# State space scan of a hybrid encoder: the steps' logarithms in the decays' exponents, and the step projection in 64 columns

## The chip, the core and the metric

The kernel runs on one core of a Trainium2 chip. The metric is the device time of one execution in microseconds (us). TensorE (PE) multiplies matrices, with the load of the stationary operand (PEld) as a separate, overlapping instruction; VectorE (DVE), ScalarE (ACT) and GpSimd (POOL) work element by element; SyncE (SP) issues the DMAs. Each engine takes its instructions in order.

## The reference, cut to what matters

One layer of an encoder over two sequences, 512 and 1024 tokens of width 1024, handled together as T = 1536 tokens. Its mixer has differential attention and a bidirectional state space scan side by side, then comes a feed-forward part. The change lies in the scan, which for each direction computes, in chunks of 128 tokens:

```
dt = softplus(dt_raw + dt_bias)                      # 16 heads per direction
xdt = x * dt
a_cum = cumsum(dt * A)                               # A = -exp(a_log)
seg = a_cum[l] - a_cum[s]
Lmat = exp(where(s <= l, seg, -inf))
y_diag = (C B^T * Lmat) @ xdt                        # per chunk and head
states, prev = scan over chunks of B^T (exp(a_cum[-1] - a_cum) * xdt)
y_off = (C @ prev) * exp(a_cum)
y = y_fwd + y_bwd + d_skip * x
```

So the weight of token s on token l in a diagonal block is the product of C·B, of the decay exp(a_cum[l] - a_cum[s]), and of the step dt[s].

## The kernel before

All products of large matrices are made of float32 numbers split into a high and a low part (`split`, `split_panel`): three matmuls (`gemm`, L164 to L166) for each product, hi·hi, hi·lo and lo·hi.

Phase one holds the normalised input hT as three blocks of 512 tokens and projects it: keys and queries (with the first sequence's attention in between), steps (`dtT`), the convolution's channels, z, and the gates. The steps are projected at L526 to L529: three blocks, each of 8 k-blocks by 3 matmuls with 32 stationary columns and 512 moving columns. Each block is copied by ACT into `dtT`.

L580 to L638 (the preamble) transpose `dtT` to token-major (L584), make `dts` = softplus in a polynomial on DVE, the cumulated sums `acm`, and the exponentials `dec`, `wst`, `eac`. Three transposes of `acm` (L627) are split into `ah`, `al` and stored to DRAM as `ac_d`; from there come four fills of `raw` (one buffer, with rows of a constant table `c_neg`) that are copied to `segr`. `segr` and a per-chunk selector `sl` are the two operands of one matmul (L749) that gives seg for four heads with a mask of -1e30 in it.

L670 to L687 run the backward direction's states over the chunks. Then L712 to L779 are the forward scan: 12 chunks by 2 groups (g) by 2 halves (hf, four heads each), 48 halves in all. In a half, for each direction: seg matmul (L749), exp on ACT (L751), one DVE operation that limits the exponential to 1 and multiplies it by the masked C·B of that direction, `cb` (L752). Then GpSimd multiplies the forward tile by `dts` (L756), four DVE operations on 128 columns multiply the backward tile by its `dts` and add the forward tile (L758), and four matmuls with 64 columns (two passes each) multiply the result by x (L762). After the halves come the skip (POOL, L763), the sums on DVE (L764, L770, L774, L775) and the norm (`finish`).

The program's order is made by a planner that takes instructions by priority as its own model of the engines says they are ready (`schedule_with_timeline_sim=True`). So work that stands later in the code is put into the gaps that the planner sees: the z projection (L694, evacuated at L691) runs in the preamble and beside the backward states, and the gates (`gates`, L424 to L435, called at L782: 14 panels by 3 blocks by 24 matmuls of 512 columns) run in the forward scan and after it. The order on each engine is then fixed. Phase two (attention of the long sequence, L785 on) reuses the memory of phase one.

Of the kernel before, what the change touches and what calls it, by code (L numbers as in the profile page):

```python
# [10 lines left out]
F32 = mybir.dt.float32  # L11
I32 = mybir.dt.int32
F32R = mybir.dt.float32r
AF = mybir.ActivationFunctionType
# [4 lines left out]
P = 128  # L19
# [59 lines left out]
def hybrid_trunk_kernel(ctx: ExitStack, tc: tile.TileContext, a: dict, y_prompt, y_sample):  # L79
# [5 lines left out]
    def f(ap):  # L85
        return ap.bitcast(F32)
# [21 lines left out]
    ac_d = dram.tile([2, 24, NH, P], F32, name="ac_d")  # L108
    f_d = dram.tile([8, 2048], F32, name="f_d")
# [58 lines left out]
    def gemm_fm(ps, w, cs, act):  # L168
        hi, lo = w
        gemm(ps, [(hi[:, k, cs], lo[:, k, cs], act[0][:, k, :], act[1][:, k, :]) for k in range(KB)])  # L170
# [5 lines left out]
    def rsqrt(r, v, t):  # L176
        """r = v ** -0.5 for positive v: a first guess from the exponent, then Newton's steps"""
        V.tensor_scalar(r.bitcast(I32), v.bitcast(I32), 1, None, op0=ALU.logical_shift_right)
        V.tensor_scalar(r.bitcast(I32), r.bitcast(I32), -1.0, 1597463007.0, op0=ALU.mult, op1=ALU.add)
        for _ in range(3):  # L180
            V.tensor_mul(t, r, r)
            V.scalar_tensor_tensor(t, t, -0.5, v, op0=ALU.mult, op1=ALU.mult)
            V.scalar_tensor_tensor(r, t, 1.5, r, op0=ALU.add, op1=ALU.mult)
# [31 lines left out]
    def operands(base, SL, h, qk, qr, got):  # L215
        """the bias table, queries and keys of a head, in steps"""
# [114 lines left out]
    def att_scale(g, zq, msq, pool, psp, ptag):  # L331
        """what the rows of attention are multiplied by: 1 / sum of exponentials and the norm"""
        n = zq.shape[-1]
        r, t = [pool.tile([P, 8, n], F32, tag=t_, name=t_, bufs=1) for t_ in ("att_r", "att_t")]
        V.reciprocal(t, zq)
        V.tensor_mul(zq, msq, t)
        V.tensor_mul(zq, zq, t)
        V.tensor_scalar(zq, zq, 1.0, EPS, op0=ALU.mult, op1=ALU.add)
        rsqrt(r[:], zq[:], msq[:])
        V.tensor_mul(r, r, t)  # L340
        ps = psp.tile([P, 512], F32, tag=ptag, name="rt")
        TE.transpose(ps[0:8 * n, 0:P], r[:].rearrange("p h j -> p (h j)"), ident)
        rt = pool.tile([P, P], F32, tag="att_rt", name="rt", bufs=1)
        V.tensor_copy(rt[0:8 * n], ps[0:8 * n, 0:P])
        store(out=r_d[g][:], in_=rt[0:8 * n])
# [14 lines left out]
    with ExitStack() as ph1:  # L360
# [143 lines left out]
        # step sizes and decays, for both directions at once  # L504
# [11 lines left out]
        wd = [wp.tile([P, KB, 32], F32R, tag=t_, name=t_) for t_ in ("whi", "wlo")]  # L516
        raw = staged(rp, [P, KB, 32], (None, w_in[:, DT0:DT0 + 32].rearrange("(a p) c -> p a c", p=P)),
                     tag="wraw")
        split(wd[0][:], wd[1][:], raw[:], "act_dve")
        dtb = sp.tile([32, 1], F32, name="dtb")  # L520
# [4 lines left out]
        dtT = dtp.tile([32, T], F32, name="dtT")  # L525
        for c in range(NCH):  # L526
            ps = acc.tile([P, 512], F32, tag="acc", name="acc")
            gemm_fm(ps[:32], wd, slice(0, 32), hT[c])
            S.activation(out=dtT[:, c * 512:(c + 1) * 512], in_=ps[:32], func=AF.Identity, bias=dtb[:, 0:1])  # L529
# [50 lines left out]
        with tc.tile_pool(name="dp", bufs=1, reuse_waits="tile") as dp, tc.tile_pool(name="dp_ps", bufs=2, space=PSUM) as dps:  # L580
            natural_log_exp()
            ps = dps.tile([P, NT, 32], F32, tag="dps", name="dt_ps")
            for t in range(NT):
                TE.transpose(ps[:, t, :], dtT[:, t * P:(t + 1) * P], ident[:32, :32])  # L584
# [4 lines left out]
            V.tensor_copy(xr, ps)  # L589
# [33 lines left out]
            ah = dp.tile([P, 3, P], F32R, name="ah")  # L623
            al = dp.tile([P, 3, P], F32R, name="al")
            for i in range(3):
                ps = dps.tile([P, P], F32, tag="dps", name="at_ps")
                TE.transpose(ps, acm[:, 4 * i:4 * i + 4, :], ident)  # L627
                S.copy(ah[:, i], ps)
                V.tensor_sub(al[:, i], ps, f(ah[:, i]))
            for i, t_ in enumerate((ah, al)):  # L630
                store(out=ac_d[i].rearrange("(i c) h l -> (c h) i l", i=3), in_=f(t_[:]))
# [80 lines left out]
        for lo_c, hi_c in SEQS:  # L712
            state = [None, None]
            for c in range(lo_c, hi_c):
                sl = sc.tile([SEGK, 2, P], F32R, tag="sl", name="sl")
                acv = [ac_d[s_, 2 * c:2 * c + 2].rearrange("d h l -> h d l") for s_ in range(2)]
# [8 lines left out]
                for g in range(2):  # L725
# [18 lines left out]
                    for hf in range(2):  # L744
                        ms = []
                        for d_ in range(2):
# [5 lines left out]
                            V.scalar_tensor_tensor(m, m, 1.0, cb[:, d_].unsqueeze(1).broadcast_to([P, 4, P]),  # L752
                                                   op0=ALU.min, op1=ALU.mult)
                            ms.append(m)
                        hh = g * 8 + hf * 4
                        G.tensor_mul(ms[0], ms[0], dts[:, c, hh:hh + 4].unsqueeze(2).broadcast_to([P, 4, P]))  # L756
                        for h in range(4):
                            V.scalar_tensor_tensor(ms[0][:, h], ms[1][:, h], dts[:, c, 16 + hh + h:17 + hh + h], ms[0][:, h],  # L758
                                                   op0=ALU.mult, op1=ALU.add)
# [99 lines left out]
    with ExitStack() as ph3:  # L859
# [43 lines left out]
        # the feed-forward's first product by Strassen's scheme in Winograd's form: seven products of half size  # L903
# [295 lines left out]
```

## Time and profile before

| | us |
|---|---|
| median of 3 runs | 3287.25 |
| lowest, highest | 3272.72, 3288.95 |
| span of the profiled execution, first to last instruction | 3277.1 |

The profiled execution's own time is given only by its span; the median lies 10.15 us above it, and that difference is carried along as what lies around the span. The span is one execution on the chip. Busy time of an engine counts the time in which it had an instruction in work; for the PE, ends of matmuls are modelled, so a PE that is busy throughout need not be at its peak. The granted clock is the TensorE clock as a share of 2.4 GHz; its lower level is 0.5 (1.2 GHz).

### The profile page before, as it was taken

The numbers are of one execution on the slowest core, as the hardware profiler recorded it, in microseconds if no ns is written. First come the engines' busy times: TensorE is split into PE (matmuls) and PEld (weight loads), VectorE is DVE, ScalarE is ACT, GpSimd is POOL, SyncE is SP. The second block draws the span as 40 slices with busy tenths as digits, with TensorE's granted clock in tenths as the row PEclk, the third lists the DMA queues.
The fourth block names the chain that finished last, engine by engine and source line by source line (L and its number), as shares of the span: only waits on it lengthen the run. The fifth ranks groups of instructions, "written<-read, shape, count | busy, mean of one in ns | idle before, by whom it ended". The sixth has DMA issues, their size and how long they took to land.

```text
span 3277.1 us, 44930 instructions
## 1 busy us (share of the span) xinstructions
PE 3068.7 (94%) x16688; PEld 2686.3 (82%) x16688; DVE 1887.9 (58%) x3048; ACT 1207.8 (37%) x2249; POOL 1086.4 (33%) x844
## 2 busy tenths in 40 slices
PE   7999999999899899999999888878999899989998
PEld 7988887889787677778888787677999899978787
DVE  5124444455238998277778765676656766642444
ACT  3013333233113333266666623243333333332343
POOL 1003332000244553167657544533333433310100
PEclk9999999999999999999999998888999999999999
DMA  4623332223553443655545146544333333363354
GB/s 145 193 97 114 112 100 76 67 74 108 174 164 124 130 133 118 200 168 172 178 144 182 39 139 221 172 132 154 98 97 106 96 100 99 110 202 94 117 166 131
DMA packets 442528, 430.00 MB, mean 131 GB/s; under 512 B 25324, under 2 KB 359617, under 8 KB 441245
## 3 DMA queue, kind: packets, MB, share of 16 engines
q1 hardware_dynamic: 442309, 427.12, 41.8%
q8 instruction: 132, 2.16, 0.3%
q14 instruction: 87, 0.71, 0.1%
HBM read 315.37 MB, written 120.05 MB: 133 GB/s over the span
## 4 chain that ended last, share of the span: by engine, by line
PE 57%; DVE 14%; DMA 12%; issue 8%; POOL 5%; ACT 4%; SPq 1%; POOLq 0%; DVEq 0%; ACTq 0%
PE acc L164 8%; PE acc L165 8%; PE acc L166 8%; PE mm L164 4%; PE mm L165 4%; PE mm L166 4%; PE d L166 3%; PE d L164 3%; PE d L165 3%; DMA wraw<-in_w_gate_up_dram 2%; DVE m L758 2%; DMA raw<-k_d 2%; DMA araw<-r_d 1%; PE s L290 1%; DVE m L752 1%
## 5 line engine op out<-in xcount | busy, mean ns | idle before, releaser
L164 PE MATMUL acc<-hT,whi 128*128 128x512 f32 (+1 forms) x1080 | 433.6, 402 | 5.8 <-ACT st L434 5.6
L165 PE MATMUL acc<-hT,whi 128*128 128x512 f32 (+1 forms) x1080 | 431.4, 399 | 0.0
L166 PE MATMUL acc<-hT,wlo 128*128 128x512 f32 (+1 forms) x696 | 273.8, 393 | 0.0
L164 PEld LDWEIGHTS acc<-hT,whi 128*128 128x128 f32 (+1 forms) x1080 | 203.6, 189 | 54.8 <-ACT st L434 6.6
L165 PEld LDWEIGHTS acc<-hT,whi 128*128 128x128 f32 (+1 forms) x1080 | 203.9, 189 | 45.6 <-issue 4.2
L296 ACT ACTIVATE pt<-pt,nm 128x1024 f32<-128x1024 f32 (+1 forms) x192 | 193.4, 1008 | 120.6 <-DVE nm L293 116.4
L293 DVE CUSTOM_DVE_ANT_0 pt<-s,tb 128x1024 f32<-128x1024 f32 (+1 forms) x192 | 197.6, 1041 | 64.5 <-PE s L291 51.2
L165 PE MATMUL acc<-wlo,hT 128*128 128x256 f32 x768 | 226.2, 295 | 0.0
L164 PE MATMUL acc<-whi,hT 128*128 128x256 f32 x768 | 224.6, 293 | 0.0
L166 PE MATMUL acc<-whi,hT 128*128 128x256 f32 x768 | 223.9, 292 | 0.0
L166 PE MATMUL d<-dhi,fl 128*128 128x512 f32 x528 | 207.6, 393 | 9.0 <-DVE fl L136 9.0
L164 PE MATMUL d<-dhi,fh 128*128 128x512 f32 x528 | 207.3, 393 | 8.1 <-DVE dlo L136 6.3
L165 PE MATMUL d<-dlo,fh 128*128 128x512 f32 x528 | 207.1, 392 | 0.0
L136 DVE TENSOR_TENSOR fl<-raw,fh 128x896 fp32r<-128x896 f32 (+1 forms) x72 | 85.9, 1195 | 199.7 <-ACT fh L135 199.7
L164 PE MATMUL mm<-op,wy 128*128 128x384 f32 x528 | 178.8, 339 | 10.2 <-ACT op L135 8.7
L166 PE MATMUL mm<-op,wy 128*128 128x384 f32 x528 | 178.7, 338 | 0.9 <-DVE wy L136 0.9
L165 PE MATMUL mm<-op,wy 128*128 128x384 f32 x528 | 178.3, 338 | 0.0
L302 POOL TENSOR_SCALAR pt<-pt,zs 128x512 f32<-128x512 f32 (+1 forms) x96 | 88.5, 921 | 253.9 <-DVE zs L300 212.6
L231 POOL TENSOR_TENSOR ql<-raw,qh 128x512 fp32r<-128x512 f32 x48 | 64.0, 1347 | 300.9 <-ACT qh L228 294.9
L166 PE MATMUL acc<-hT,whi 128*128 128x512 f32 x384 | 159.1, 414 | 0.0
L164 PEld LDWEIGHTS acc<-whi,hT 128*128 128x128 f32 x768 | 148.4, 193 | 8.9 <-issue 8.0
L135 ACT CAST whi<-wraw 128x1024 fp32r<-128x1024 f32 (+2 forms) x76 | 75.8, 1024 | 215.4 <-PE acc L166 99.6
(344 smaller groups left out, 8696.0 us busy)
## 6 DMA issues: line engine op xcount, KB each, us to landing
wraw<-in_w_in_dram SPq DMA_DIRECT2D x60, 512.0 KB
wraw<-in_w_gate_up_dram SPq DMA_DIRECT2D x92, 256.0 KB
raw<-ff_d SPq DMA_DIRECT2D x48, 448.0 KB
wr<-in_w_gate_up_dram SPq DMA_DIRECT2D x80, 256.0 KB
ff_d<-c SPq DMA_DIRECT2D x88, 192.0 KB
g_d<-st SPq DMA_DIRECT2D x48, 256.0 KB
xg<-xs_d SPq DMA_DIRECT2D x48, 256.0 KB
gt<-g_d SPq DMA_DIRECT2D x48, 256.0 KB
```

The lines of the kernel that those rows point to most:

```text
L135: S.copy(hi, raw)
L136: V.tensor_sub(lo, raw, f(hi))
L164: TE.matmul(ps, ah, bh, start=(i == 0), stop=False)
L165: TE.matmul(ps, ah, bl, start=False, stop=False)
L166: TE.matmul(ps, al, bh, start=False, stop=(i == n - 1))
L231: G.tensor_sub(q_l[:, s_], q_r[:, s_], f(q_h[:, s_]))
L290: TE.matmul(sps[:, ks], qh[m][:, qs], km[m][:, ks], start=True, stop=False)
L293: V.tensor_tensor_reduce(out=pt[:], in0=sps[:], in1=tb[:, off:off + SL], scale=-1.0, scalar=3.0e38, op0=ALU.add, op1=ALU.min, accum_out=nm ...
L296: S.activation(out=pt, in_=pt, func=AF.Exp, bias=nm[:, m:m + 1], scale=-1.0, accum_out=(z0, zs[:, 0:1])[m])
L302: G.tensor_scalar(pm[1][:, cb], pm[1][:, cb], zs[:, 1:2], 0.0, op0=ALU.mult, op1=ALU.add)
L752: V.scalar_tensor_tensor(m, m, 1.0, cb[:, d_].unsqueeze(1).broadcast_to([P, 4, P]), op0=ALU.min, op1=ALU.mult)
L758: V.scalar_tensor_tensor(ms[0][:, h], ms[1][:, h], dts[:, c, 16 + hh + h:17 + hh + h], ms[0][:, h], op0=ALU.mult, op1=ALU.add)
```

## The change

The steps' logarithm is taken into the exponent: exp(a_cum[l] - (a_cum[s] - log dt[s])) already holds the factor dt[s]. A second table `ad_d` (a_cum minus log dt, `acl`) is stored beside `ac_d`, and the selector `sl` is filled from it. The multiplications by `dts` in the scan (L756, L758) go; the two masked tiles are added by one DVE operation. The limit of L752 is 3.0e38 instead of 1. The preamble gets the logarithm with one correction step, and three more transposes and two more stores. The step projection has the high and low parts of the weights side by side as 64 stationary columns, so that a block takes 16 matmuls instead of 24; the two halves are added after the transposes (which now also adds the product lo·lo).

```diff
+    ad_d = dram.tile([2, 24, NH, P], F32, name="ad_d")
...
-        wd = [wp.tile([P, KB, 32], F32R, tag=t_, name=t_) for t_ in ("whi", "wlo")]
+        wd = wp.tile([P, KB, 64], F32R, tag="whi", name="wd")
...
-        split(wd[0][:], wd[1][:], raw[:], "act_dve")
-        dtb = sp.tile([32, 1], F32, name="dtb")
+        split(wd[:, :, 0:32], wd[:, :, 32:64], raw[:], "act_dve")
+        dtb = sp.tile([64, 1], F32, name="dtb")
+        V.memset(dtb, 0.0)
...
-        dtT = dtp.tile([32, T], F32, name="dtT")
+        dtT = dtp.tile([64, T], F32, name="dtT")
         for c in range(NCH):
             ps = acc.tile([P, 512], F32, tag="acc", name="acc")
-            gemm_fm(ps[:32], wd, slice(0, 32), hT[c])
-            S.activation(out=dtT[:, c * 512:(c + 1) * 512], in_=ps[:32], func=AF.Identity, bias=dtb[:, 0:1])
+            for i, (k, part) in enumerate((k, part) for k in range(KB) for part in hT[c]):
+                TE.matmul(ps[:64], wd[:, k, :], part[:, k, :], start=i == 0, stop=i == 2 * KB - 1)
+            S.activation(out=dtT[:, c * 512:(c + 1) * 512], in_=ps[:64], func=AF.Identity, bias=dtb[:, 0:1])
...
-            ps = dps.tile([P, NT, 32], F32, tag="dps", name="dt_ps")
+            ps = dps.tile([P, NT, 64], F32, tag="dps", name="dt_ps")
             for t in range(NT):
-                TE.transpose(ps[:, t, :], dtT[:, t * P:(t + 1) * P], ident[:32, :32])
+                TE.transpose(ps[:, t, :], dtT[:, t * P:(t + 1) * P], ident[:64, :64])
...
-            V.tensor_copy(xr, ps)
+            V.tensor_copy(xr, ps[:, :, 0:32])
+            V.tensor_add(xr, xr, ps[:, :, 32:64])
...
-            ah = dp.tile([P, 3, P], F32R, name="ah")
-            al = dp.tile([P, 3, P], F32R, name="al")
-            for i in range(3):
-                ps = dps.tile([P, P], F32, tag="dps", name="at_ps")
-                TE.transpose(ps, acm[:, 4 * i:4 * i + 4, :], ident)
-                S.copy(ah[:, i], ps)
-                V.tensor_sub(al[:, i], ps, f(ah[:, i]))
-            for i, t_ in enumerate((ah, al)):
-                store(out=ac_d[i].rearrange("(i c) h l -> (c h) i l", i=3), in_=f(t_[:]))
+            acl = dp.tile([P, NT, 32], F32, name="acl")
+            V.tensor_scalar(t1, dts, 1.0e-30, 0.0, op0=ALU.max, op1=ALU.add)
+            S.activation(out=t2, in_=t1, func=AF.Ln)
+            S.activation(out=u, in_=t2, func=AF.Exp, scale=-1.0)
+            V.tensor_mul(u, u, t1)
+            V.scalar_tensor_tensor(t2, u, -1.0, t2, op0=ALU.add, op1=ALU.add)
+            V.tensor_sub(acl, acm, t2)
+            ah = dp.tile([P, 2, 3, P], F32R, name="ah")
+            al = dp.tile([P, 2, 3, P], F32R, name="al")
+            for j, a_ in enumerate((acm, acl)):
+                for i in range(3):
+                    ps = dps.tile([P, P], F32, tag="dps", name="at_ps")
+                    TE.transpose(ps, a_[:, 4 * i:4 * i + 4, :], ident)
+                    S.copy(ah[:, j, i], ps)
+                    V.tensor_sub(al[:, j, i], ps, f(ah[:, j, i]))
+            for j, d__ in enumerate((ac_d, ad_d)):
+                for i, t_ in enumerate((ah, al)):
+                    store(out=d__[i].rearrange("(i c) h l -> (c h) i l", i=3), in_=f(t_[:, j]))
...
-                acv = [ac_d[s_, 2 * c:2 * c + 2].rearrange("d h l -> h d l") for s_ in range(2)]
+                acv = [ad_d[s_, 2 * c:2 * c + 2].rearrange("d h l -> h d l") for s_ in range(2)]
...
-                            V.scalar_tensor_tensor(m, m, 1.0, cb[:, d_].unsqueeze(1).broadcast_to([P, 4, P]),
+                            V.scalar_tensor_tensor(m, m, 3.0e38, cb[:, d_].unsqueeze(1).broadcast_to([P, 4, P]),
                                                    op0=ALU.min, op1=ALU.mult)
                             ms.append(m)
-                        hh = g * 8 + hf * 4
-                        G.tensor_mul(ms[0], ms[0], dts[:, c, hh:hh + 4].unsqueeze(2).broadcast_to([P, 4, P]))
-                        for h in range(4):
-                            V.scalar_tensor_tensor(ms[0][:, h], ms[1][:, h], dts[:, c, 16 + hh + h:17 + hh + h], ms[0][:, h],
-                                                   op0=ALU.mult, op1=ALU.add)
+                        V.tensor_add(ms[0], ms[0], ms[1])
```

## Rows read from the trace of the kernel before

**Rows 1.** The page's head and its line of engine totals

```profile
span 3277.1 us, 44930 instructions
PE 3068.7 (94%) x16688; PEld 2686.3 (82%) x16688; DVE 1887.9 (58%) x3048; ACT 1207.8 (37%) x2249; POOL 1086.4 (33%) x844
```

**Rows 2.** Busy time by stretch of the span, columns in the first line

```profile
core 0: us, PE busy (x) PEld busy (x) DVE busy (x) ACT busy (x) POOL busy (x), PEclk, DMA share, GB/s
580.00:640.00 60.00, 60.00 (x282) 49.94 (x281) 27.67 (x18) 19.20 (x26) 0.51 (x9) 1.00 0.18 53
850.00:860.00 10.00, 5.40 (x13) 3.34 (x14) 1.39 (x2) 0.00 (x0) 4.12 (x5) 0.50 0.69 209
900.00:940.00 40.00, 40.00 (x250) 31.87 (x248) 11.73 (x17) 2.39 (x4) 19.74 (x19) 1.00 0.61 199
970.00:1303.00 333.00, 305.38 (x1444) 240.09 (x1444) 301.27 (x538) 113.81 (x284) 171.27 (x126) 0.96 0.41 129
1350.00:1400.00 50.00, 36.55 (x147) 28.27 (x146) 13.00 (x15) 14.40 (x19) 9.62 (x8) 0.93 0.84 230
1450.00:1500.00 50.00, 48.99 (x279) 41.86 (x278) 40.97 (x65) 34.31 (x55) 44.47 (x30) 1.00 0.62 190
```

**Rows 3.** Waits in the forward scan, 960 to 1310 us: in all, times, longest

```profile
PEld yd L762 <- DVE m L758: 23.1, 17, 2.6
PE yd L762 <- DVE m L758: 18.8, 12, 2.2
DVE m L758 <- POOL m L756: 15.4, 16, 2.9
```

**Rows 4.** Groups by line and shape, 960 to 1310 us: busy us, mean ns | idle before

```profile
L758 DVE SCALAR_TENSOR_TENSOR m<-m,dts 128x128 f32<-128x128 f32 x192 | 104.9, 603 | 15.7 <-POOL m L756 15.4
L752 DVE SCALAR_TENSOR_TENSOR m<-m,cb 128x512 f32<-128x512 f32 x96 | 80.3, 865 | 4.6 <-ACT m L751 4.2
L756 POOL TENSOR_TENSOR m<-m,dts 128x512 f32<-128x512 f32 x48 | 66.5, 1390 | 108.2 <-DVE m L752 86.8 <-PE yt_ps L705 13.0 <-PE yo_ps L768 6.8
L775 DVE TENSOR_TENSOR yz<-yz 128x512 f32<-128x512 f32 x24 | 21.2, 883 | 0.1
```

**Rows 5.** The tile m: durations ns min/median/max, first and last start

```profile
L758 DVE SCALAR_TENSOR_TENSOR m<-m,dts x192: 335/344/2557, 975.5 to 1300.9; 128x128 f32<-128x128 f32 x192
L752 DVE SCALAR_TENSOR_TENSOR m<-m,cb x96: 676/685/2878, 971.5 to 1298.5; 128x512 f32<-128x512 f32 x96
```

**Rows 6.** Matmuls of line L166 alone in the forward scan

```profile
970.00:1303.00 333.00, 105.06 (x250) 48.86 (x251) 0.96 0.41 129
```

**Rows 7.** ACT's timeline where gates run alone: start us, us

```profile
1309.02 0.59 ACT L434 COPY st<-acc 128x512 f32<-128x512 f32 x1 [2.67 <-PE acc L166]
1314.46 0.59 ACT L434 COPY st<-acc 128x512 f32<-128x512 f32 x1 [4.85 <-PE acc L166]
```

**Rows 8.** Step projection, 540 to 575 us, by line and shape

```profile
L164 PE MATMUL acc<-hT,whi 128*32 128x512 f32 x24 | 10.5, 437 | 0.1
```

**Rows 9.** Waits of the PE, 545 to 590 us

```profile
PE rt L342 <- DVE att_r L340: 3.7, 1, 3.7
```

**Rows 10.** Preamble and backward states, 780 to 965 us, by line and shape

```profile
L691 ACT ACT_TABLE_LOAD x4 | 5.1, 1283 | 4.8 <-issue 4.7
L627 PE MATMUL at_ps<-ident,acm 128*128 128x128 f32 x3 | 0.8, 271 | 0.0
L621 DVE TENSOR_TENSOR wst<-wst,dts 128x384 f32<-128x384 f32 x1 | 0.6, 558 | 0.3 <-ACT wst L620 0.3
L622 ACT ACTIVATE eac<-acm 128x384 f32<-128x384 f32 x1 | 0.5, 526 | 3.9 <-DVE acm L613 3.9
```

**Rows 11.** The chain that ended last, 820 to 860 us: start us, us, what

```profile
825.23 2.73 DMA ac_d<-al
...
847.15 6.19 DMA xg<-xs_d
```

**Rows 12.** Waits of the PE, 775 to 970 us

```profile
PE st_ps L661 <- POOL xw L659: 7.5, 1, 7.5
```

## Prediction

> **What bounds the kernel now.** The page comes first. TensorE is busy for 94% of the span and VectorE for 58% [rows 1], and over the whole program nothing would be won by taking work off VectorE. The view by stretch says where that is otherwise. In the forward scan, 970 to 1303 us, VectorE is busy for 301.27 of 333 us, the PE for 305.38, GpSimd for 171.27, and the granted clock is 0.96 [rows 2]. Both engines are nearly full, because the planner puts the gates' matmuls into the scan. The PE loses time in two ways there: 333 - 305.4 = 27.6 us idle, and a clock of 0.96, which is 2 x 0.04 = 8% of the stretch (26.6 us) at 1.2 GHz doing half the work, 13.3 us. Packed, its work would take 333 - 27.6 - 13.3 = 292 us. The view of waits says who holds it: weight loads and matmuls of the yd line wait for L758 on VectorE, 23.1 and 18.8 us (the two overlap), and L758 itself waits 15.4 us for GpSimd's L756 [rows 3]. So the scan is paced by the chain exp, L752, L756, L758, yd, and what a quicker VectorE can give is the 41 us that the PE loses, not the VectorE time itself.
>
> The Trainium skill, "Perfetto Trace Analysis", section Identifying the Most-Contended Engine, calls matmul busy time a bad measure of headroom and takes the weight loads' busy share in its place. In this trace that share is 240.09 / 333 = 72% against 49.94 / 60 = 83% where the PE has no gap [rows 2]; by it the packed length would be 289 us and the possible gain 44 us instead of 41.
>
> **The scan.** Removed from VectorE: 192 L758, 104.9 us busy [rows 4]. Their median is 344 ns and their mean 603 [rows 4, 5], so much of this is stretched by something running beside them. Added: 48 adds of 128x512 with both inputs in SBUF. The trace has the same shape at 685 ns undisturbed (L752's median [rows 5]) and 883 ns as they came (L775's mean [rows 4]): 33 to 42 us, and I take 38. The 96 L752 stay, with another constant. They were busy for 80.3 us against 96 x 0.685 = 65.8 undisturbed, 14.5 us too long. GpSimd loses the 48 L756, 66.5 of its 171.3 us, 39% [rows 2, 4]. If the stretching goes with GpSimd's time in work, 39% of 14.5, 5.7 us, goes too (bounds 0 and 14.5). VectorE then has 301.3 - 104.9 + 38 - 5.7 = 229 us. ACT's work in the scan does not change.
>
> The Trainium skill, "SBUF — State Buffer", section Who interferes with whom, says that a VectorE instruction with two SBUF inputs and a GpSimd instruction that reads SBUF block each other for a whole instruction. The medians and means above agree in direction. By that rule the add that comes in is open to the same blocking as what goes out.
>
> What does the PE make of it? With VectorE at 229 of some 300 us, 76%, the nearest stretches are 1450 to 1500 (VectorE 82%, PE busy 98%, clock 1.00) and 900 to 940 (VectorE 29%, PE 100%, clock 1.00) [rows 2]. The scan has more small dependent matmuls than either, so I take 97.5% busy and a clock of 0.98: 292 / (0.975 x 0.98) = 306 us, a gain of 27. The bounds are 0 (the PE keeps its waits) and 41 (none left). Gates that no longer fit into a shorter scan run after it, at 5.44 us for a block of 24 matmuls [rows 7]; they are counted in the 292, so moving them costs nothing as long as the PE stays packed.
>
> **The step projection.** 3 blocks by 8 matmuls go. A matmul with 32 stationary columns took 10.5 / 24 = 0.44 us busy, and three lines of 24 took 31 us of overlapping busy time [rows 8]; a block of 24 full-width ones runs at 5.44 / 24 = 0.227 us each [rows 7]. The 24 that go are worth 24 x 0.227 = 5.4 us if they all lie on the path. Some don't: the PE waits 3.7 us for the end of the attention (att_r) in the middle of them [rows 9], and a shorter block before that wait only makes it longer. The third block lies behind it. I take 3 us, with bounds 0 and 5.4. The weights' split, the `dtb` loads and the evacuations keep their number; the added memset of `dtb` and the sixty-four rows of the copies are not on the PE, and their cover is the same 3.7 us wait.
>
> **The preamble.** The new work is, on VectorE, one add and four operations of the logarithm at about 0.558 us, 2.8 us; on ACT, Ln and Exp at 0.526, 1.1 us, and up to two more table loads at 1.283, 2.6 us, since z's Silu evacuations lie between; on the PE three transposes at 0.271, 0.8 us [rows 10]; three copies and three subtractions behind them, at most another 3 x (0.526 + 0.558) = 3.3 us by the longer shapes; and two stores of some 2.7 us to landing, which overlap [rows 11]. In one row that is 2.8 + 1.1 + 2.6 + 0.8 + 3.3 + 2.7 = 13.3 us. It would all stand on the chain if the `ad_d` stores were issued ahead of the reads of `ac_d`: SP takes its queue in order, and behind them wait the `segr` fills, z's stores and the scan's first x (landed after 6.19 us [rows 11]). What covers it is the z projection on the PE, which the planner places there, and the backward states that follow are PE-full as well, 40.00 of 40 [rows 2]; z's matmuls that move ahead leave room behind. What is not covered is what the planner misjudges. That is visible now: the PE waits 7.5 us for the first st_ps [rows 12], and its clock is 0.50 from 850 to 860 [rows 2]. I take a loss of 2 us, with bounds 0 and 13.3.
>
> **Behind the scan** the PE is idle for 50 - 36.55 = 13.5 us from 1350 to 1400, where phase two's loads arrive [rows 2]. An earlier end of the scan frees memory earlier, while more gates remain to cover the loads. But phase two's first panels need the weight buffers that the gates hold. I take 0, with bounds of 10 us gained and 6 lost.
>
> **The sum.** 27 + 3 - 2 + 0 = 28 us. Against its own execution, 3277.1 - 28 = 3249 us of span. The median of the runs lies 10.15 us above that span, so 3287.25 - 28 = 3259 us. A difference within 0.5%, 16.4 us (3271 to 3304), is about what a measurement of this kernel can't tell from no change.
>
> **Rivals.**
>
> *All of the headroom.* The PE is packed in the scan, the projection gives its full 5.4 us and the shorter scan covers the transition: 41 + 5 + 10 = 56 us, 3231. For it speaks that the stretches after and before the scan run at clock 1.00; against it, the yd matmuls depend on each half's add, which comes last.
>
> *The chain, not the load.* The PE's waits are set by the length of the chain in a half and by the planner's order, and not by how full VectorE is: without L756 the chain loses 1.4 us a half but exp, two L752 and the add remain in a row behind each seg matmul. The planner's order, made for a shorter chain, may be as tight as before, and the PE keeps 20 of its 27.6 us idle and most of the slow clock. Then the gain in the scan is some 8 us, and with 3 - 2 the time is 3278, no change. For it: VectorE's waits for a predecessor are short and many (15.4 us in 16 [rows 3]). Against it: VectorE at 90% leaves no slack to catch up, at 76% it does.
>
> The same page, in the same section, takes the engine with the highest occupancy as the one to work on. By matmul busy time that is the PE at 92% here, and the change takes nothing off it in the scan; this rival is where that leads.
>
> *Too few gates in the scan.* The scan holds 250 / 8 = 31 blocks of gates now [rows 6], 31 x 5.44 = 170 us, so its own PE work is 292 - 170 = 122 us. Let the scan shrink to VectorE's 229 us and its present 333 - 301.3 = 31.7 us not busy, 260 us. If k blocks remain in it, 31 - k follow at 5.44 us. It breaks even with 333 at 31 - 73 / 5.44 = 17.6 blocks and is slower by 0.5% below 14.6, three fewer. Packed, 260 us has room for (260 - 122) / 5.44 = 25. With 13 blocks, stage and rest take 260 + 18 x 5.44 = 358 us, 25 more than now; with 3 - 2 that is 3311, slower. It would also show as a clock below 0.90, as from 850 to 860, where the PE had been half idle [rows 2]. Against it: the gates are there to be taken whenever the scan's matmuls are not ready, and up to 1303 us the PE was kept at 92%.
>
> **How the numbers follow.** The forecast, 3259 with 3243 to 3270 as its own range (scan gain 17 to 38 with the other bounds partly used), has 0.57. All of the headroom has 0.14, the chain 0.18, too few gates 0.11. Faster by over 0.5% is the forecast and the first rival, less a little of the forecast's edge: 0.70. Within 0.5%: 0.19. Slower: 0.11. The range for 8 in 10 reaches from the first rival's 3231 through the chain's 3278 to that case with the preamble's uncovered 13 us, 3290, and leaves out most of too few gates: 3231 to 3290.
>
> **What would show it.** In the changed kernel's scan: VectorE's busy time per half down by about a quarter; no L756; the mean of L752 below 865 ns; the adds between 0.69 and 0.88 us; the PE's waits for the add well under 42 us; a clock of 0.98 or more; the last half's yd some 35 to 70 us earlier, with more than ten blocks of gates behind it. In the preamble: the first st_ps's wait still near 7.5 us. The prediction is wrong if the PE's idle time in the scan and the gates together stays above 20 us, if the clock stays at 0.96, or if the time won there comes back as idle PE between the gates and the first heads of phase two.

## The result and the profile after

The changed kernel takes 3243.65 us (median of 4 runs, 3229.39 to 3245.51) against 3285.62 us before on the same chip (3272.72 to 3288.95): a ratio of 0.9869, 95% interval 0.9842 to 0.9895. It is faster by about 42 us; forecast were 28, with 3259 as the time and 3231 to 3290 as the range; the forecast's own, narrower range, 3243 to 3270, only just holds it. The profiled execution spans 3243.3 us, 33.8 less than the one before; it took 3245.1 us in all. So only 1.8 us lie around a span, and the 10 us by which the median lay above the span of before were the difference between two executions.

The view by stretch of the changed kernel, for the forward scan from its first seg matmul to its last yd, and for scan and gates together (columns as in [rows 2]; after each engine's busy time stands its number of instructions, then the granted clock, the DMA's share and its GB/s):

```profile
968.10:1258.00 289.90, 284.75 (x1423) 226.29 (x1422) 253.27 (x393) 112.34 (x282) 116.31 (x78) 1.00 0.48 145
968.10:1327.60 359.50, 351.54 (x1718) 280.93 (x1717) 269.61 (x419) 130.60 (x318) 124.12 (x82) 1.00 0.50 151
```

The same two stretches of the kernel before, cut at the same instructions:

```profile
969.70:1302.50 332.80, 305.18 (x1446) 239.98 (x1445) 300.99 (x537) 114.11 (x284) 171.57 (x126) 0.96 0.41 129
969.70:1373.00 403.30, 369.93 (x1713) 292.06 (x1712) 318.95 (x563) 131.13 (x319) 178.78 (x130) 0.96 0.43 135
```

The scan is 42.9 us shorter and holds nearly as many matmuls (1423 against 1446, one block of gates fewer). The PE's idle time fell from 27.6 to 5.2 us and the granted clock rose from 0.96 to 1.00. Before, the PE lost 27.6 + 13.3 = 41 us of the scan; now it loses 5.

The PE's waits in the changed scan (in all, times, longest):

```profile
PE yd L772 <- DVE m L769: 1.4, 3, 0.7
PE cb_ps L753 <- DVE yo L779: 1.3, 2, 1.1
```

Of the 18.8 us that PE matmuls waited for L758 [rows 3], 1.4 us are left, for the add in its place. VectorE's groups in the changed scan, by line and shape (L766 is L752 of before, L769 the new add, L785 and L784 are L775 and L774):

```profile
L766 DVE SCALAR_TENSOR_TENSOR m<-m,cb 128x512 f32<-128x512 f32 x96 | 85.4, 921 | 5.9 <-ACT m L765 5.7
L769 DVE TENSOR_TENSOR m<-m 128x512 f32<-128x512 f32 x48 | 41.9, 875 | 0.4
L784 DVE TENSOR_TENSOR yz<-yz,yb 128x512 f32<-128x512 f32 x20 | 21.8, 1091 | 0.2
L785 DVE TENSOR_TENSOR yz<-yz 128x512 f32<-128x512 f32 x23 | 21.6, 940 | 0.1
L780 DVE TENSOR_TENSOR yz<-yz,yo 128x512 f32<-128x512 f32 x19 | 16.3, 857 | 0.1
```

L766 is slower on average than L752 was (921 against 865 ns [rows 4]), although GpSimd has a third less to do. The forecast had it falling; it is taken up below.

Milestones of the changed kernel: first dt transpose (L587), first seg (L763), and first and last evacuation of gates (L435). A row gives the shortest, median and longest duration in ns, then the first and last start in us:

```profile
L587 PE MATMUL dt_ps<-ident,dtT x12: 222/222/272, 776.1 to 776.8; 64*128 64x64 f32 x12
L763 PE MATMUL seg<-segr,sl x96: 392/399/800, 968.1 to 1246.1; 119*128 119x512 f32 x96
L435 ACT COPY st<-acc x48: 563/586/622, 501.8 to 1327.6; 128x512 f32<-128x512 f32 x48
```

and the same of the kernel before:

```profile
L584 PE MATMUL dt_ps<-ident,dtT x12: 220/222/243, 779.4 to 780.1; 32*128 32x32 f32 x12
L749 PE MATMUL seg<-segr,sl x96: 389/402/803, 969.7 to 1290.8; 119*128 119x512 f32 x96
L434 ACT COPY st<-acc x48: 563/586/612, 501.6 to 1373.0; 128x512 f32<-128x512 f32 x48
```

So the first dt transpose, which follows the steps' projection, comes 3.3 us earlier; the preamble with the backward states takes 192.0 instead of 190.3 us, 1.7 more; the gates' end comes 45.4 us earlier. Of these, 33.8 are left at the end of the span. The other 11.6 were lost in stages that the change doesn't touch. The last matmul of attention's output comes 39.4 us earlier (1838.1 against 1877.5). The matmuls that use `wy`, in a product behind the attention, begin 36.6 us earlier and end 33.3 earlier (after, then before):

```profile
L165 PE MATMUL mm<-op,wy x528: 336/337/687, 2165.1 to 2849.5; 128*128 128x384 f32 x176
```

```profile
L164 PE MATMUL mm<-op,wy x528: 336/337/687, 2201.7 to 2882.8; 128*128 128x384 f32 x176
```

### The profile page after: what moved, and what is told of

The parts are those of the page before. It is cut to its first block, busy times and chain, and to the rows that moved or that the text cites. A ratio compares the mean times of both kernels' runs of the same rounds, so it can differ in the third digit from the quotient of the medians.

```text
span 3243.3 us, 44646 instructions
## 1 busy us (share of the span) xinstructions
PE 3049.5 (94%) x16667; PEld 2677.0 (83%) x16667; DVE 1842.6 (57%) x2913; ACT 1209.3 (37%) x2255; POOL 1034.0 (32%) x796
## 4 chain that ended last, share of the span: by engine, by line
PE 63%; DMA 12%; DVE 10%; issue 6%; POOL 4%; ACT 3%; SPq 1%; POOLq 0%; ACTq 0%; DVEq 0%
PE acc L165 9%; PE acc L167 9%; PE acc L166 9%; PE mm L165 5%; PE mm L167 5%; PE mm L166 5%; PE d L167 4%; PE d L166 3%; PE d L165 3%; DMA araw<-r_d 1%; DMA raw<-k_d 1%; DMA wraw<-in_w_gate_up_dram 1%; DMA gt<-g_d 1%; PE yd L772 1%; PE st_ps L675 1%
## 5 line engine op out<-in xcount | busy, mean ns | idle before, releaser
L165 PE MATMUL acc<-hT,whi 128*128 128x512 f32 x1056 | 420.9, 399 | 2.8 <-ACT st L435 2.8
L166 PE MATMUL acc<-hT,whi 128*128 128x512 f32 x1056 | 416.1, 394 | 0.0
L167 PE MATMUL acc<-hT,wlo 128*128 128x512 f32 x672 | 263.7, 392 | 0.0
L165 PEld LDWEIGHTS acc<-hT,whi 128*128 128x128 f32 x1056 | 198.5, 188 | 47.9 <-issue 5.5
L166 PEld LDWEIGHTS acc<-hT,whi 128*128 128x128 f32 x1056 | 198.6, 188 | 42.2 <-issue 3.6
L166 PE MATMUL acc<-wlo,hT 128*128 128x256 f32 x768 | 225.2, 293 | 0.0
L166 PE MATMUL d<-dlo,fh 128*128 128x512 f32 x528 | 207.1, 392 | 0.0
L166 PE MATMUL mm<-op,wy 128*128 128x384 f32 x528 | 178.3, 338 | 0.0
L136 ACT CAST fh<-raw 128x896 fp32r<-128x896 f32 (+1 forms) x72 | 70.8, 983 | 227.7 <-PE d L166 212.7
L167 PE MATMUL acc<-hT,whi 128*128 128x512 f32 x384 | 155.5, 405 | 0.0
## 6 DMA issues: line engine op xcount, KB each, us to landing
ff_d<-c SPq DMA_DIRECT2D x88, 192.0 KB
```

The source lines that it names most:

```text
L136: S.copy(hi, raw)
L165: TE.matmul(ps, ah, bh, start=(i == 0), stop=False)
L166: TE.matmul(ps, ah, bl, start=False, stop=False)
L167: TE.matmul(ps, al, bh, start=False, stop=(i == n - 1))
```

## The experiments

These numbers are worked out for each scan. **The PE's loss**: the stretch from the first seg to the end of the last yd, less the PE's busy time, plus (1 - clock) x the stretch, since the share 2 x (1 - clock) ran at half speed. The clock has two digits, so a loss is good to about 1.5 us. **The stretch of VectorE**: for the tile m's operations and the three additions and products on yz with two SBUF inputs, busy time less count times the undisturbed duration (0.685 us for 128x512, 0.344 for 128x128 [rows 5]; 0.681 for the yz operations, the medians of their rows). For the kernel before that is (104.9 - 66.0) + (80.3 - 65.8) + (21.2 - 16.3) and 6.4 for the other two, 65 us. Two more columns give this sum otherwise: for the tile m's operations alone, and for all of VectorE's lines that lengthen, which adds the product yz<-yz,yrs, the copies to sl and the operations yss, yrst and yrs on one column (0.754, 0.282, 0.150, 0.219 and 0.160 us undisturbed, the medians in the kernel before). Each run was compared with the kernel before on its own chip.

| kernel | ratio to before (95%) | scan us | PE's loss us | VectorE busy us | stretch us | on m alone us | all lines us |
|---|---|---|---|---|---|---|---|
| before | 1 | 333 | 41 | 301 | 65 | 53 | 72 |
| changed | 0.9869 (0.9842 to 0.9895) | 290 | 5 | 253 | 46 | 29 | 56 |
| a_again | 0.9870 (0.9853 to 0.9888) | 296 | 11 | 255 | 49 | 28 | 58 |
| e_scan | 0.9910 (0.9884 to 0.9936) | 297 | 13 | 255 | 51 | 27 | 58 |
| f_pd | 0.9888 (0.9866 to 0.9910) | 299 | 13 | 256 | 51 | 33 | 58 |
| f_p | 0.9907 (0.9884 to 0.9929) | 305 | 14 | 282 | 46 | 39 | 55 |
| f_d | 0.9943 (0.9922 to 0.9964) | 318 | 25 | 274 | 66 | 42 | 78 |
| g_pool | 0.9956 (0.9942 to 0.9971) | 316 | 31 | 279 | 69 | 46 | 83 |
| g_add | 0.9853 (0.9837 to 0.9869) | 281 | 7 | 242 | 47 | 21 | 73 |
| g_dve | 0.9898 (0.9879 to 0.9916) | 311 | 11 | 275 | 46 | 32 | 53 |
| s_act | 0.9924 (0.9907 to 0.9941) | 310 | 20 | 281 | 49 | 40 | 55 |
| h_raw2 | 0.9872 (0.9854 to 0.9889) | 296 | 12 | 256 | 49 | 31 | 58 |
| e_dt64 | 0.9994 (0.9982 to 1.0005) | 335 | 42 | 299 | 63 | 49 | 70 |
| b_both | 0.9831 (0.9807 to 0.9855) | 281 | 7 | 242 | 46 | 21 | 72 |

### Taking the cut apart: f_p, f_d, f_pd

The kernel before, with the first, the second, or both of these edits:

```diff
-                        G.tensor_mul(ms[0], ms[0], dts[:, c, hh:hh + 4].unsqueeze(2).broadcast_to([P, 4, P]))
...
-                        for h in range(4):
-                            V.scalar_tensor_tensor(ms[0][:, h], ms[1][:, h], dts[:, c, 16 + hh + h:17 + hh + h], ms[0][:, h],
-                                                   op0=ALU.mult, op1=ALU.add)
+                        V.tensor_add(ms[0], ms[0], ms[1])
```

> The kernel before without GpSimd's multiplication L756 (the forward step sizes are left out of the diagonal blocks); the four L758 stay. Theory 'load' (VectorE's own work and the time GpSimd blocks it pace the scan; what is won is capped by the 41 us that the PE loses there): 48 of 126 GpSimd instructions go; at 67 us of stretching over 126, 0.53 us each, VectorE loses 25 us of stretching and 15 us of waiting for L756, so the scan is 25 to 35 us shorter, the time about 3255. Rival 'chain' (the row of instructions in a half sets the pace): a hop of 1.39 us goes from each of 48 halves, 67 us, more than the cap, so all of the 41 us: about 3245. Rival 'blocking is nothing': only the 15 us of waits: about 3270.

> The kernel before with one add of 128x512 in place of the four L758 (the backward step sizes are left out); GpSimd's L756 stays. Load: VectorE loses 48 x (4 x 0.344 - 0.685) = 33 us of its own work, GpSimd blocks as before, so the scan is some 25 to 33 us shorter, the time about 3257. Chain: only 0.7 us of the row in a half goes and GpSimd's hop stays in it, so at most 15 us: about 3270. If load and chain are both wrong and L756 alone was the cause, no change: about 3285.

> The kernel before with both: no L756, one add for the four L758 (step sizes left out of the diagonal blocks); preamble and step projection as before. Load and chain alike: the scan reaches the cap, 41 to 43 us shorter, about 3243, and the two halves of the cut don't add up (each alone over half of it). Rival 'order' (the planner's other order after the longer preamble made part of the gain): clearly less than 42 us, 3255 or more.

Measured: 3251.15, 3260.72 and 3244.66 us, against 3280.44 before on that chip: 29, 20 and 36 us. The scan of each, by stretch; first without L756:

```profile
969.60:1275.00 305.40, 293.96 (x1442) 231.94 (x1442) 281.64 (x537) 111.96 (x280) 117.06 (x78) 0.99 0.47 139
```

with one add for the four L758:

```profile
972.70:1290.40 317.70, 302.40 (x1462) 239.36 (x1461) 274.33 (x394) 113.09 (x284) 177.79 (x126) 0.97 0.45 135
```

with both:

```profile
971.80:1270.30 298.50, 291.07 (x1423) 230.10 (x1422) 255.51 (x393) 111.62 (x280) 116.77 (x78) 0.98 0.46 141
```

The two halves don't add up, so there is a cap, as both theories had it. But each theory is right in one run and misses the other: "load" has f_p's scan (27 us shorter, of 25 to 35) and misses f_d's (15, of 25 to 33); "chain" has f_d's (at most 15) and misses f_p's (all of 41). By the time of the whole, f_d's 3261 lies nearer to load's 3257 than to chain's 3270, and f_p's 3251 between its 3255 and 3245. Without L756 VectorE is busy for 282 of 305 us, 92%, more than before, and the PE's loss falls to 14 us. With the add it is busy for 274 of 318, 86%, and the loss is 25. How full VectorE is does not decide. What f_d kept is most of the stretch: its lines show where (compare the 0.685 us undisturbed).

```profile
L752 DVE SCALAR_TENSOR_TENSOR m<-m,cb 128x512 f32<-128x512 f32 x96 | 87.9, 946 | 6.5 <-ACT m L751 6.3
L757 DVE TENSOR_TENSOR m<-m 128x512 f32<-128x512 f32 x48 | 52.9, 1103 | 18.6 <-POOL m L756 18.2
```

With fewer VectorE instructions to meet, each is held longer: the 65 us of stretch stayed at 66 (on m alone 53 became 42). f_pd's 299 us against the changed kernel's 290 looked like an effect of the order (the rival in its expectation), but the runs below take that back.

### The same scan three times: a_again and e_scan

e_scan is the changed kernel with the step projection of before, a_again the changed kernel once more.

> The changed kernel with the step projection as before (32 columns, three matmuls): the scan's and the preamble's part alone. By the milestones the projection's end came 3.3 us earlier: 3247. If the 24 matmuls were all on the path: 5.4 us, 3249. If the scan's part depended on what went before it, the difference is larger than 8 us either way.

> The changed kernel once more, beside the three below on one chip. The cut alone (no L756, one add, old preamble and projection) took 298 us for the scan at a clock of 0.98, the changed kernel 290 at 1.00, the changed kernel with the old projection, whose scan has the same code, 297 at 0.98. If that is chance of the clock, this run's scan lies between 290 and 298 us and its time 36 to 43 us below before; if the projection does something for the scan, 290 again.

The scan took 296 us in a_again and 297 in e_scan, both in the same code as the changed kernel's 290. The changed kernel alone gave 290 and 296, so a difference of 6 us is chance, most of it the clock; e_scan and f_pd lie 1 and 3 us beyond. The stretch of e_scan from its first seg:

```profile
978.60:1275.20 296.60, 289.53 (x1423) 228.94 (x1422) 254.91 (x393) 111.48 (x279) 115.54 (x78) 0.98 0.47 142
```

A clock of 0.98 on 290 us of PE work is 6 us. So f_pd's scan is that of the changed kernel too: the cut makes the scan's gain, the preamble's order nothing that shows. e_scan's 3250.96 us miss the expected 3247 by 4 us; its first evacuation of gates stands at 505.7 us instead of 501.6, before anything that was changed, so that much is not the projection's; its own runs lie between 3243 and 3263 us.

### Work without the row, and the row without the work: g_pool, g_add

```diff
                         V.tensor_add(ms[0], ms[0], ms[1])
+                        dum = sc.tile([P, 512], F32, tag="dum", name="dum", bufs=1)
+                        G.tensor_mul(h3(dum[:]), h3(x_g[:]), hb(dec, c, 0, g))
```

```diff
-                        V.tensor_add(ms[0], ms[0], ms[1])
+                        G.tensor_add(ms[0], ms[0], ms[1])
```

> The changed kernel with one more GpSimd multiplication of 128x512 in each half, into a tile that nobody reads: GpSimd's work and its blocking of VectorE are as in the kernel before, but the GpSimd step does not stand in the row of a half. Theory 'load and blocking': VectorE gets 48 x 0.53 = 25 us of stretching back, 253 to 278 us, and the scan loses 10 to 25 us against the changed kernel. Theory 'hop' (what cost the PE its time was waiting for GpSimd's result within a half): within 8 us of the changed kernel, VectorE's busy time up by as much as above all the same.

> The changed kernel with the add of the two tiles on GpSimd instead of VectorE: VectorE has 42 us less work, but every half has a GpSimd step of some 1.4 us just before its yd matmuls. Load: VectorE falls to some 215 us and the PE is no worse off than in the changed kernel, 0 to 5 us faster. Hop: the GpSimd step stands in the row again and the PE waits for it, 10 to 25 us slower than the changed kernel.

g_pool took 3265.38 us against a_again's 3237.46 on the same chip, 28 us more (the profiled spans differ by 23); g_add 3233.07. The scan of a_again, then of g_pool:

```profile
970.60:1266.80 296.20, 288.56 (x1423) 228.45 (x1422) 254.83 (x393) 112.07 (x282) 119.86 (x78) 0.99 0.47 142
```

```profile
969.00:1284.60 315.60, 297.53 (x1422) 233.28 (x1422) 279.25 (x393) 112.21 (x282) 176.69 (x122) 0.96 0.44 134
```

and the instructions that its added line stretched (1033 and 1002 ns on average, where the changed kernel has 921 and 875, a_again 916 and 881):

```profile
L766 DVE SCALAR_TENSOR_TENSOR m<-m,cb 128x512 f32<-128x512 f32 x96 | 96.2, 1033 | 5.3 <-ACT m L765 5.1
L769 DVE TENSOR_TENSOR m<-m 128x512 f32<-128x512 f32 x48 | 48.0, 1002 | 0.5
L771 POOL TENSOR_TENSOR dum<-xg,dec 128x512 f32<-128x512 f32 x44 | 61.6, 1400 | 23.6 <-DMA xg<-xs_d 23.1
```

VectorE runs the same instructions as in the changed kernel, nobody waits for the dummy, and yet some 20 (against a_again) to 26 us (against the changed kernel) of the scan's gain are gone: the idle time is back at 18 us and the clock at 0.96. One other way is closed by the waits: that the dummies make GpSimd's own results late for the PE. For those the PE waits 3.0 us, against 1.5 in a_again; the line of g_pool, then of a_again:

```profile
PE st_ps L675 <- POOL xw L673: 3.0, 2, 2.1
```

```profile
PE st_ps L675 <- POOL xw L673: 1.5, 2, 0.9
```

The scan of g_add, with as much GpSimd work and with the GpSimd step in every half's row:

```profile
970.20:1251.40 281.20, 277.25 (x1394) 222.06 (x1393) 242.05 (x346) 112.48 (x282) 171.38 (x124) 0.99 0.48 147
```

The PE waits for that step by all of this:

```profile
PE yd L772 <- POOL m L769: 0.5, 1, 0.5
```

So the hop costs nothing here, and the theory "hop" is out. But the time for which GpSimd holds VectorE up does not explain g_add by itself either. VectorE is busy for 242 us, not for the 215 that were expected: 33 us of its own work went, and over all lines the stretch rose from 58 us to 73, as much as in the kernel before, while the PE loses 7 us and not 41. The lines of g_add show what is held:

```profile
L766 DVE SCALAR_TENSOR_TENSOR m<-m,cb 128x512 f32<-128x512 f32 x96 | 86.3, 928 | 5.6 <-ACT m L765 5.5
L780 DVE TENSOR_TENSOR yz<-yz,yo 128x512 f32<-128x512 f32 x19 | 24.2, 1275 | 0.5
L734 DVE CAST sl<-slr 119x256 fp32r<-119x256 f32 x10 | 10.8, 1076 | 0.1
L196 DVE TENSOR_TENSOR yrs<-yrs,yrst 128x1 f32<-128x1 f32 x11 | 9.0, 819 | 0.4
```

In the changed kernel these four take 921, 857, 624 and 553 ns on average. What grew in g_add lies outside the row of a half; on the operations on m, which stand between exp and yd, the stretch is 21 us, all on L766, since the add is no longer VectorE's. Over the table's fourteen profiles the PE's loss goes with that column: with up to 33 us on m it is 5 to 13, with 39 to 46 it is 14 to 31, with 49 and 53 it is 42 and 41. Neither the stretch of all lines nor VectorE's busy share orders them so. This was read off afterwards, and no run was made to test it. The scan of g_add is also shorter because it holds a block of gates less (1394 matmuls); scan and gates together take 357.4 us, against 359.5 in the changed kernel and 364.7 in a_again.

### VectorE's own work against blocking: g_dve, s_act

g_dve adds a VectorE instruction to each half of the changed kernel; s_act takes L756 of the kernel before from GpSimd to ACT:

```diff
+                        dum = sc.tile([P, 1], F32, tag="dum", name="dum", bufs=1)
+                        V.reduce_sum(dum, x_g, axis=mybir.AxisListType.X)
```

```diff
-                        G.tensor_mul(ms[0], ms[0], dts[:, c, hh:hh + 4].unsqueeze(2).broadcast_to([P, 4, P]))
+                        for h in range(4):
+                            S.activation(out=ms[0][:, h], in_=ms[0][:, h], func=AF.Copy, scale=dts[:, c, hh + h:hh + h + 1])
```

> The changed kernel with one more VectorE instruction in each half, a sum over x (128x512, one SBUF input) that nobody reads, some 0.6 us, 29 us in all. Theory 'load' (how full VectorE is decides): VectorE comes to about 283 us, as with the extra GpSimd step (279 us, scan 316), so the scan takes 310 us or more, the time 3258 or more. Theory 'late against the plan' (the order counts each instruction's own time, so what makes the PE wait is only the time for which GpSimd blocks VectorE beyond that): the planner sees the added work, the blocking stays at some 50 us, and the scan takes at most 303 us, as without L756 (VectorE 282 us, scan 305), the time 3240 to 3248.

> The kernel before with the multiplication L756 on ACT, as four scaled copies of 128 columns (some 0.37 us each): the hop in the row of a half stays, VectorE's own work stays, only GpSimd's 48 instructions go. Late against the plan: the blocking falls from 67 to some 50 us and the scan is 25 to 30 us shorter, as with L756 left out; the time 3250 to 3257. If the hop in the row matters, or ACT with 70 us more becomes the bound: no better than before, 3270 or more.

g_dve took 3240.71 us, as "late against the plan" had it, but its scan is 311 us, as "load" had it, and not 303. The stretch says why:

```profile
969.50:1280.60 311.10, 303.20 (x1490) 239.78 (x1489) 275.21 (x437) 115.09 (x283) 118.98 (x80) 0.99 0.45 140
```

The added instruction, over the whole kernel (durations and starts as above):

```profile
L771 DVE TENSOR_REDUCE dum<-xg x48: 667/674/689, 945.1 to 1264.6; 128x1 f32<-128x512 f32 x48
```

The scan holds 1490 matmuls instead of 1423, nearly three blocks of gates more: the order made for this kernel, with 48 x 0.674 = 32 us more of VectorE work in it, fills the longer scan, and scan and gates together take 360.6 us, where the changed kernel takes 359.5. The PE's loss is 11 us, as in a_again. In g_pool, with VectorE as busy (279 us), it holds 1422: the order has no more in the scan than the changed kernel's, and the loss is 31. At the same busy share of VectorE (88.5% in both) the one costs some 9 us of the kernel's time by the ratios to before (0.9898 against a_again's 0.9870; the intervals overlap, and the bare medians, from two chips, differ by 3), the other 28. The added sum itself is not held up (667 to 689 ns), and the stretch on m is 32 us against g_pool's 46.

s_act took 3250.05 us, 26 less than before on its chip, with all of the kernel's VectorE work and the hop in place:

```profile
969.60:1279.10 309.50, 298.29 (x1431) 236.16 (x1431) 281.26 (x538) 168.64 (x471) 114.69 (x78) 0.97 0.44 136
```

Its scan is 23 us shorter (25 to 30 expected), its stretch is down to 49 us, and about half of the PE's loss is gone. Its loss of 20 us stays above that of f_p, which has no step at all in that place; whether ACT's 61 us or the longer row cost these 6 us was not tried.

### The projection alone, the fills, and both small edits: e_dt64, h_raw2, b_both

e_dt64 is the kernel before with the projection's part of the diff. h_raw2 gives the fills of segr in the changed kernel's preamble a second buffer, b_both has that and g_add's edit:

```diff
                     raw = staged(dp, [SEGK, 1024], (slice(0, 12), acv[0]), (slice(12, 24), acv[1]),
-                                 (slice(24, SEGK), a["c_neg"][d_][:, os_]))
+                                 (slice(24, SEGK), a["c_neg"][d_][:, os_]), bufs=2)
```

> The kernel before with the step projection in 64 columns alone. By the milestones of the changed kernel 3.3 us: the first dt transpose at 776 instead of 779 us, the time 3 us below before, which the interval of a ratio may not tell from nothing. If it does something for the scan as well, more than 8 us.

> The changed kernel with two buffers instead of one for the four fills of segr in the preamble. There the PE waits 8.9 us for the first st_ps, whose x comes behind the serial fills, and the clock falls to 0.61 in the ten us that follow. If the serial fills hold the first x, that wait shrinks to 0 to 4 us and the time is 5 to 9 us below the changed kernel. If the transfers themselves are what takes long (x landed 8 us after its issue, amid the fills), the wait stays at 7 to 9 us and the time is the same.

> The changed kernel with both small edits that did not lose: the add on GpSimd and two buffers for the segr fills. If their parts stand side by side: the scan at 281 us and the first st_ps 8 us earlier, the time 3228 to 3234, below the changed kernel's 3237 to 3244. If what is won before the scan is given back behind it, as with two buffers alone: 3233 to 3237.

e_dt64 took 3273.23 us against 3276.46, with an interval that holds 1. From the first evacuation of gates to the first dt transpose it is 275.5 us (503.1 to 778.6) against 277.8 before; in the changed kernel 274.3 and in a_again 275.4. The projection is worth 2.3 to 3.5 us in these traces, too little for the kernel's time to show.

In h_raw2 the first st_ps comes at 845.1 us instead of a_again's 855.2, and the PE's wait there is 5.5 instead of 9.0 us, but the scan starts only 6.7 us earlier (963.9 against 970.6), attention ends 4.8 earlier, and the time is the same: 3239.04 against 3237.46. The wait of 5.5 us lies between the two expectations, 0 to 4 and 7 to 9, so the serial fills hold the first x only in part. A second buffer moves the start, and most of that does not reach the end.

b_both took 3220.84 us against 3276.46, 0.9831 (0.9807 to 0.9855), where the changed kernel had 0.9870 on another chip. Its scan:

```profile
967.00:1248.10 281.10, 277.31 (x1394) 222.14 (x1393) 241.88 (x346) 112.56 (x282) 173.28 (x124) 0.99 0.47 147
```

That is g_add's scan. The time is below both expectations, of which the lower began at 3228. It is the fastest version found, 12 to 13 us below the changed kernel by the ratios. As with the others, the end of the kernel follows its scan only in part, and how much of the 13 us belongs to which edit is not settled.

## Why the prediction was right, point by point

**What bounds the scan: right in the sum, half right in the cause.** The 41 us that the PE loses was the size of the prize, and nearly all of it was won: 41 went to 5 in the profiled scan, 11 in the repeat. The prediction ascribed the loss to VectorE being full. The runs show that its busy share does not decide: g_dve at 88.5% costs some 9 us, g_pool at 88.5% costs 28, f_p at 92% is faster than f_d at 86%. What is shown is that GpSimd's work beside VectorE costs the PE time: taken out it wins 26 us of loss in f_p and 20 in s_act, put back where nobody waits for it, in g_pool, it costs (31 - 11) us of loss for (69 - 49) of stretch, 25 over all lines. It is not a price for every microsecond of stretch, since g_add has 73 us of it over all lines and loses 7. That the stretch on m is what counts fits all fourteen profiles and is not tested. VectorE work that the planner counted cost little in g_dve, and about half of itself in f_d (16 us of loss won for 33 of work), which sits on top of the full blocking. Why counted work is cheap is argued from the matmul counts above, not shown: the order makes room for it.

**The scan's term was mis-sized: 27 forecast, 43 measured.** The step that failed is "97.5% busy and a clock of 0.98"; it was 284.75 / 289.9 = 98.2% and 1.00, and one block of gates (5.4 us) stands behind the scan now. With the gates, the stretch is 43.8 us shorter. In the repeat the clock was 0.99 and the scan 36.6 us shorter, between the forecast and this. That a shorter scan would leave more gates behind it, as the prediction and its third rival had it, hardly happened: 1423 against 1446 matmuls. That the total came out near the forecast is partly luck: the 16 us won beyond the forecast in the scan and the 12 lost behind it work against each other.

**VectorE's time: 229 forecast, 253 measured.** It fell by 16%, where the prediction's signs had about a quarter. The add came out at the upper bound, 41.9 us of 33 to 42. The step that failed is the stretch: the sum took L758's 38.9 us of it away with L758, and had L752's fall with GpSimd's time, but that rose from 14.5 to 85.4 - 65.8 = 19.6 us. Stretch goes by the GpSimd instructions more than by the VectorE ones: 65 us for 126 GpSimd instructions before, 0.52 us each; 46 for 78 after, 0.59; 69 for 122 in g_pool, 0.57; 46 for 78 in f_p, 0.58; over all lines 0.55 to 0.75 each in all fourteen profiles, g_add among them with 0.59. What GpSimd can't take from L758 it takes from L752 and the yz lines. By that, 48 instructions less were worth 25 us of stretch, not 5.7, if the average held for those that go; 18 were seen, 16 over all lines. An instruction less took off 0.3 to 0.6 us, by either sum, in the pairs that differ by them (before and f_p, f_d and f_pd, g_pool and a_again).

The rule of the Trainium skill, "SBUF — State Buffer", section Who interferes with whom, that the two block each other for a whole instruction, agrees: the median of L766 is 685 ns and its longest took 2871, and the added L769, which the prediction held open to the same, averages 875 with a median of 684. The weight loads' busy share, of the Trainium skill, "Perfetto Trace Analysis", section Identifying the Most-Contended Engine, went from 72 to 226.29 / 289.9 = 78% in the scan, and its bound of 44 us was as good as the 41. The advice in that section to work on the engine with the highest occupancy, which the prediction sets beside its second rival, would not have told g_dve from g_pool.

**The projection: right**, 3 forecast, 2.3 to 3.5 by the milestones. **The preamble: right**, 2 lost forecast, 1.7 measured; the first st_ps's wait went from 7.5 to 8.9 us [rows 12], so the cover by z's matmuls held.

**Behind the scan: 0 forecast, 12 lost** in the profiled pair (6.0 from the gates to the last attention output, 2.8 from there to the first matmul with `wy`, 3.3 along those matmuls, and 0.5 regained after them), outside the bound of 6. From the last gate's evacuation to the last attention output the PE is idle for 32.9 us instead of 27.4, so some of the time won did come back as idle PE, as one of the prediction's signs of being wrong had it, but only 5.5 of 45 us; in the repeat it is 26.8. The repeat ended its gates 7.7 us later than the changed kernel's first profile (1335.3 against 1327.6), and its attention only 0.5 us later (1838.6 against 1838.1); so what is won or lost before the attention does not pass through it one for one. What holds it there was not tried. It stays open, as does the spread of 16 us between executions of one kernel, which hides anything below about 8 us in the end-to-end time.

**The rivals.** "All of the headroom" is what the scan did; the total stayed short of its 3231 because the transition lost 12 us instead of giving 10. "The chain" had the PE keep 20 us idle, and it kept 5; that the hop was not what cost the time is shown by g_add. "Too few gates" did not arise.

## What to carry to other kernels

Where GpSimd and VectorE both work on SBUF tiles beside a full TensorE, an instruction taken off GpSimd gives VectorE time back: 0.3 to 0.6 us each here, on whichever VectorE instruction is met. By the fourteen profiles, though no run tested it, this is worth most where the instructions met stand in the row between the matmuls that feed them and the matmuls that wait for them. In the two runs that compare them, VectorE work that the order was planned with cost some 9 us, and GpSimd work that blocks VectorE 28; so look at mean against median of VectorE's groups, line by line, and not at its busy share. And size the gain of such a cut by what the bounding engine loses in the stage, idle time and slow clock together; then expect that some of it is not seen at the end.

## What the runs showed of the hardware

- A GpSimd instruction that nobody waits for cost the kernel 28 us in 48 instances (g_pool; 23 by the profiled spans), beside 20 us of blocking of VectorE in the profile, 25 over all lines.
- A VectorE sum over 128x512 with one SBUF input took 667 to 689 ns in all 48 instances (g_dve), while operations of that size with two SBUF inputs, 685 ns at the median, took up to 2871 (changed kernel).
- The same scan code ran at a granted clock of 1.00, 0.99, 0.98 and 0.98 in the four profiles that hold it (changed, a_again, e_scan, h_raw2), worth up to 6 us.
- ACT's scaled copy of 128 columns took 392 ns on average in s_act (192 of them, 61.4 us busy), with ACT busy for 168.64 of the scan's 309.5 us.
